# Splitting FFN weights with fewer, wider VectorE instructions, and a third seven-product pair in the long down products

## Chip, cores and metric

The kernel runs on one core of one Trainium2 chip, as one launch. The metric is the device time of that launch in microseconds (us). A run executes the program and reports its time; one more execution is recorded by the hardware profiler, and every profile row below is from such an execution.

## What is computed

A two-layer decoder trunk on 256 tokens of width 2048, in float32: a dilated-window attention layer and a latent-attention layer, each followed by a SwiGLU feed-forward block (FFN), all with RMSNorm and residuals. The change concerns the FFN, which runs once per layer:

```python
D_MODEL = 2048; SEQ = 256; FFN_HIDDEN = 5632
def swiglu(xn, w_gu, w_down):                 # xn (256, 2048), w_gu (2048, 11264), w_down (5632, 2048)
    g, u = jnp.split(xn @ w_gu, 2, axis=-1)
    return (jax.nn.silu(g) * u) @ w_down
# each layer:  h = h + attention(rms_norm(h));  h = h + swiglu(rms_norm(h, ffn_norm_g), w_gu, w_down)
```

## The kernel before

**Products in two parts.** TensorE (PE) multiplies in `float32r`, which keeps fewer bits than float32. Every weight tile `raw` is therefore split: ScalarE (ACT) rounds it to `hi` (`nc.scalar.copy` with a cast), VectorE (DVE) forms the residue `lo = raw - hi`. The activations are stored in the same way, transposed, as `xT` and `hT`. A product of a 128x128 block of x with a 128x512 block of w is three matmuls: x_hi w_hi, x_hi w_lo, x_lo w_hi (`mul` in `mixed`, lines 689 to 691). A line of the profile that names `halve` (L167 and L168) is this split in the FFN; L157 and L158 are the same split in the attention layers.

**Units and the stream.** `WeightStream` holds a list of units. In the FFN, a unit is a `raw` tile of [128, 2048]: two k blocks (rows of the weight) times two column blocks of 512, in the order b12, b11, b22, b21. Two transfers of 512 KB on the SP queue fill it. `ws.next()` hands out a unit and, before that, emits the split of the unit two places ahead (`ahead=2`) and the loads after it. There are three buffers each of `raw`, `hi` and `lo`. A `hi` buffer comes free when PE has done its last matmul with it, a `raw` buffer when DVE has read it last.

**Eight or seven products.** One unit meets a 2x2 block of x (two k blocks, two token halves), so it is a 2x2 by 2x2 block product. An "eight" unit takes eight `mul`, 24 matmuls. A "seven" unit uses a Winograd form with seven `mul`, 21 matmuls: three take the unit's own `hi` and `lo`, four take `th` and `tl`, the split of four combinations of its blocks, which DVE makes in place in `raw` (lines 185 to 188). `th` and `tl` have one buffer each. On the x side, `sums` makes the matching combinations, once for each k pair (`forms` for the gate/up products, `forms_h` for the down products). Four PSUM banks `pb` collect the shared products; after the last seven unit, line 721 combines them into the tiles `left` and `right`.

**Stages.** An FFN is worked in three parts of its hidden width, with 16, 16 and 12 blocks of 128 (`FFN_PARTS`). In a part, for each four blocks (`j`), `mixed` computes the gate and up products over eight k pairs `kp` = 0 to 7; all but the first of a layer have seven units at kp 2, 4 and 6 (`SEVEN`), and there are 20 such products in the program. Then line 739 adds the accumulators `la` (gate) and `ra` (up) to `left` and `right` ("gate add", "up add"), line 745 is the silu on ACT, line 747 multiplies on DVE, and `turned`, one unit later, transposes the result on PE into `hT` (line 405) and calls `sums` on the pairs that need it. `la` and `ra` have two buffers in PSUM together, so the next product's first matmul waits for the gate add. After the gate/up products of the two long parts come two long down products each (`mixed` again, eight k pairs, eight in the program), with seven units at kp 2 and 5; the short part's down product has none and uses other code.

**Order.** The code is written in program order and a scheduler of the language sets the order on each engine; each engine then works its own list strictly in that order and waits on semaphores of the others. An instruction that waits holds up all that stand behind it on its engine.

In what follows S2, S4 and S6 are the seven units of a gate/up product by their kp, E3, E5 and E7 the eight units between them, E0' and E1' the first two of the next product and S2' its first seven unit.

Of the kernel before, what the change touches and what calls it, by code (L numbers as in the profile page):

```python
# [48 lines left out]
SEVEN_DOWN = {16: (2, 5), 12: ()}  # L49
# [38 lines left out]
class WeightStream:  # L88
# [81 lines left out]
    def split_blocks(self, raw, form):  # L170
# [14 lines left out]
        tt(out=b22, in0=b22, in1=b12, op=ALU.subtract)  # L185
        tt(out=b12, in0=b12, in1=b11, op=ALU.subtract)
        tt(out=b11, in0=b11, in1=b22, op=ALU.add)  # L187
        tt(out=b21, in0=b21, in1=b11, op=ALU.subtract)
        for i in (slice(0, 1024), slice(1024, 2048)):
            self.halve(th[:, i], tl[:, i], raw[:, i])  # L190
# [32 lines left out]
def kernel(ctx, tc, consts, x, attn_norm_g, ffn_norm_g, a_w_qkv, a_w_o, kv_norm_g,  # L223
# [206 lines left out]
    def across(r, name):  # L430

        dg = tmp.tile([P, S], F32, tag="diag", name="diag", bufs=1)
        for t in range(NT):
            nc.vector.tensor_scalar(out=dg[:, t * P:(t + 1) * P], in0=ident, scalar1=r[:, t:t + 1],
                                    scalar2=None, op0=ALU.mult)
# [205 lines left out]
    def ffn(xT, rstd, finish):  # L641

        with tc.tile_pool(name="ffn", bufs=1) as fp:
# [11 lines left out]
            forms_h = fp.tile([P, 2, 2, 3, P], F32R, name="forms_h")  # L655

            def sums(x, kp, d):
# [7 lines left out]
                for i, x_, y_, op in ((0, a21, a22, ALU.add), (1, g[:, 0], a11, ALU.subtract),  # L665
                                      (2, a11, a21, ALU.subtract), (3, a12, g[:, 1], ALU.subtract)):
# [12 lines left out]
            def mixed(X, pairs, seven, sums_of, left, right):  # L679
# [5 lines left out]
                pb = None  # L685
# [289 lines left out]
```

## Time and profile before

| | |
|---|---|
| median of 3 runs (lowest, highest) | 2673.95 us (2673.07, 2676.16) |
| span of the profiled execution, first to last instruction | 2672.9 us |
| mean granted TensorE clock | 0.998 |
| PE busy | 2655.3 us, 99% of the span |
| DVE busy | 2020.8 us, 76% |
| ACT busy | 1295.8 us, 48% |

The profiler gives the profiled execution as its span; its time with what lies around the span is not listed apart, and the median of the runs is 1.05 us above the span. PE's busy share says little about stalls, since matmuls are pipelined: a 128x512 matmul is listed with 390 ns while the next one starts 227 ns after it. So PE is read here by starts, not by busy time. The same holds in a small way for DVE and ACT: an instruction's listed time overlaps the next one's start when the next does not need its result. The FFNs lie at about 950 to 1670 us and 1920 to 2672 us of the span.

### The profile page before, as it was taken

To read this page: it belongs to the slowest core of one execution; us is meant where nothing else is said; L and a number is where in the kernel's file an instruction comes from. 1 tells how busy PE (TensorE), PEld (TensorE's weight loads), DVE (VectorE), ACT (ScalarE), POOL (GpSimd) and SP (SyncE) were. 2 spreads that over 40 slices of the span, in tenths; PEclk is the share of its full clock that TensorE was granted. 3 is DMA by queue.
4 is the path that set the end of the run, shared out by engine and by line. 5 is a ranking of instruction groups with operands and counts; after the bars stand their busy time and mean duration, and the time that the engine had idled before them with its cause. 6 is when DMAs were issued, how large, how long until landed. Compare 5 with 4: busy or idle time off the path is not lost.

```text
span 2672.9 us, 32983 instructions
## 1 busy us (share of the span) xinstructions
PE 2655.3 (99%) x12938; PEld 2228.0 (83%) x12938; DVE 2020.8 (76%) x2758; ACT 1295.8 (48%) x1649; POOL 24.9 (1%) x28
## 2 busy tenths in 40 slices
PE   9999999999999999999999999999999999999998
PEld 7888888888888888888888888888888888888887
DVE  5676577477477668988998896588579978997985
ACT  5444444434444445544554454565445544554553
POOL 0000000000000000000000000000000000000000
PEclk9999999999999999999999999999999999999999
DMA  7545545554555555566566756444555576657663
GB/s 271 190 158 171 192 159 173 189 174 164 174 183 165 198 188 190 184 210 221 185 211 211 227 175 203 157 143 140 177 180 189 189 230 199 217 188 222 204 215 133
DMA packets 308091, 504.20 MB, mean 189 GB/s; under 512 B 13960, under 2 KB 117088, under 8 KB 307552
## 3 DMA queue, kind: packets, MB, share of 16 engines
q1 hardware_dynamic: 302960, 492.64, 55.2%
q0 software_dynamic: 4352, 8.39, 1.7%
q8 instruction: 101, 1.65, 0.3%
q10 hardware_dynamic: 624, 1.07, 0.1%
q14 instruction: 54, 0.44, 0.0%
HBM read 491.57 MB, written 2.10 MB: 185 GB/s over the span
## 4 chain that ended last, share of the span: by engine, by line
PE 87%; DVE 6%; DMA 3%; issue 2%; ACT 2%; SPq 0%; POOL 0%; ACTq 0%; DVEq 0%; POOLq 0%
PE acc L451 14%; PE acc L689 10%; PE acc L690 10%; PE acc L691 10%; PE acc L471 8%; PE acc L470 8%; PE acc L472 8%; PE acc L454 7%; DVE lo L168 2%; PE bank L689 2%; PE bank L691 2%; PE bank L690 2%; DMA raw<-in_ffn_w_gu_dram 1%; DMA raw<-in_ffn_w_down_dram 1%; PE bank L566 1%
## 5 line engine op out<-in xcount | busy, mean ns | idle before, releaser
L158 DVE TENSOR_TENSOR lo<-raw,hi 128x1024 fp32r<-128x1024 f32 (+2 forms) x450 | 515.7, 1166 | 347.3 <-ACT hi L157 331.3
L157 ACT CAST hi<-raw 128x1024 fp32r<-128x1024 f32 (+2 forms) x450 | 432.6, 1006 | 550.0 <-PE acc L451 297.4
L167 ACT CAST hi<-raw 128x1024 fp32r<-128x1024 f32 (+1 forms) x404 | 443.8, 1130 | 384.3 <-PE acc L691 146.4
L168 DVE TENSOR_TENSOR lo<-raw,hi 128x1024 fp32r<-128x1024 f32 (+1 forms) x404 | 526.2, 1321 | 110.0 <-ACT hi L167 108.8
L689 PE MATMUL acc<-hi,xT_f 128*128 128x512 f32 x988 | 387.2, 392 | 0.4 <-DVE gate L739 0.4
L691 PE MATMUL acc<-hi,xT_f 128*128 128x512 f32 x988 | 385.4, 390 | 0.0
L690 PE MATMUL acc<-lo,xT_f 128*128 128x512 f32 x988 | 385.0, 390 | 0.0
L451 PE MATMUL acc<-xT_a,hi 128*128 128x512 f32 x1536 | 379.4, 395 | 0.0
L451 PEld LDWEIGHTS acc<-xT_a,hi 128*128 128x128 f32 x1536 | 281.6, 188 | 53.8
L689 PEld LDWEIGHTS acc<-hi,xT_f 128*128 128x128 f32 x988 | 185.5, 188 | 41.8 <-issue 2.5
L167 ACT CAST th<-raw 128x1024 fp32r<-128x1024 f32 x152 | 154.0, 1049 | 133.4 <-DVE raw L187 122.3
L691 PEld LDWEIGHTS acc<-hi,xT_f 128*128 128x128 f32 x988 | 185.5, 188 | 39.1
L690 PEld LDWEIGHTS acc<-lo,xT_f 128*128 128x128 f32 x988 | 185.6, 188 | 38.2
L454 PEld LDWEIGHTS acc<-xT_a,lo 128*128 128x128 f32 x1536 | 196.9, 191 | 7.6
L454 PE MATMUL acc<-xT_a,lo 128*128 128x256 f32 x1536 | 199.2, 283 | 0.0
L168 DVE TENSOR_TENSOR tl<-raw,th 128x1024 fp32r<-128x1024 f32 x152 | 180.5, 1221 | 12.6 <-ACT th L167 12.4
L689 PE MATMUL acc<-hi,hT 128*128 128x512 f32 x400 | 156.4, 391 | 1.5 <-DVE gate L739 1.0
L691 PE MATMUL acc<-hi,hT 128*128 128x512 f32 x400 | 155.9, 390 | 0.0
L690 PE MATMUL acc<-lo,hT 128*128 128x512 f32 x400 | 155.8, 390 | 0.0
L471 PE MATMUL acc<-lo,xT_a 128*128 128x512 f32 x384 | 150.6, 392 | 0.8 <-DVE lo L158 0.8
L472 PE MATMUL acc<-hi,xT_a 128*128 128x512 f32 x384 | 150.9, 393 | 0.0
L470 PE MATMUL acc<-hi,xT_a 128*128 128x512 f32 x384 | 150.8, 393 | 0.0
(274 smaller groups left out, 3942.6 us busy)
## 6 DMA issues: line engine op xcount, KB each, us to landing
raw<-in_ffn_w_gu_dram SPq DMA_DIRECT2D x352, 512.0 KB, 4.5
raw<-in_a_w_qkv_dram SPq DMA_DIRECT2D x143, 1024.0 KB, 4.9
raw<-in_ffn_w_down_dram SPq DMA_DIRECT2D x128, 512.0 KB, 5.0
raw<-in_ffn_w_down_dram SPq DMA_DIRECT2D x24, 1024.0 KB, 5.1
raw<-in_a_w_o_dram SPq DMA_DIRECT2D x16, 1024.0 KB, 5.0
raw<-in_b_w_o_dram SPq DMA_DIRECT2D x16, 1024.0 KB, 5.1
raw<-in_b_w_kv_b_dram SPq DMA_DIRECT2D x8, 1024.0 KB, 5.3
raw<-in_b_w_q_b_dram SPq DMA_DIRECT2D x8, 768.0 KB, 4.5
```

The lines of the kernel that those rows point to most:

```text
L157: nc.scalar.copy(out=h, in_=src)
L158: nc.vector.tensor_tensor(out=l, in0=src, in1=h.bitcast(F32), op=ALU.subtract)
L167: self.nc.scalar.copy(out=hi, in_=src)
L168: self.nc.vector.tensor_tensor(out=lo, in0=src, in1=hi.bitcast(F32), op=ALU.subtract)
L451: mm(out=acc[:, i, :], lhsT=sl(hi, kk), rhs=xT[:, k0 + kk, :], start=first and kk == 0, stop=False)
L454: mm(out=acc[:, i, 0:S], lhsT=sl(lo, kk), rhs=xT[:, k0 + kk, 0:S], start=False, stop=last and kk == nk - 1)
L470: mm(out=acc[:, t, :ncol], lhsT=xh, rhs=rhs(hi, kk), start=st, stop=False)
L471: mm(out=acc[:, t, :ncol], lhsT=xh, rhs=rhs(lo, kk), start=False, stop=False)
L472: mm(out=acc[:, t, :ncol], lhsT=xl, rhs=rhs(hi, kk), start=False, stop=sp)
L689: mm(out=out, lhsT=xh, rhs=wh, start=st, stop=False)
L690: mm(out=out, lhsT=xh, rhs=wl, start=False, stop=False)
L691: mm(out=out, lhsT=xl, rhs=wh, start=False, stop=sp)
```

## The change

It has five edits.

1. `split_blocks`: an eight unit is split in one piece of 2048 columns instead of two of 1024. In a seven unit DVE first adds b11 to b12 in place (line 177), then all 2048 columns are split (before, the 1536 of b11, b22 and b21). One subtraction of 512 (line 182) and one of 1024 columns with a broadcast operand (line 183) make the three combinations, which are split in one piece of 1536 into `th` and `tl` (before, four combinations in two pieces of 1024).
2. `mixed`: of the seven `mul`, four now use the unit's own `hi` and `lo` and come first, and three use `th` and `tl`.
3. The combination after the last seven unit takes three instructions instead of four (two of 512 columns, one of 1024); `gate` has three slots of 512 in place of `gate` with two and `u2`.
4. `SEVEN_DOWN` for the long down products is (2, 4, 6) instead of (2, 5). `sums` is called for one more pair in each long part; one of its subtractions has its operands exchanged.
5. `across` builds its diagonal in `R` instead of a tile of its own.

On DVE, at the third seven unit of a gate/up product (the fourth product of a layer's first part; raw_8680 before and raw_8611 after are that S6, raw_8721 and raw_8649 the E7 behind it; line 168 is `halve` in both kernels), before:

```order
L168 TENSOR_TENSOR lo_8783<-raw_8680,hi_8782 128x1536
L185 TENSOR_TENSOR raw_8680<-raw_8680 128x512
L186 TENSOR_TENSOR raw_8680<-raw_8680 128x512
L168 TENSOR_TENSOR lo_8821<-raw_8721,hi_8820 128x1024
L187 TENSOR_TENSOR raw_8680<-raw_8680 128x512
L168 TENSOR_TENSOR lo_8821<-raw_8721,hi_8820 128x1024
L188 TENSOR_TENSOR raw_8680<-raw_8680 128x512
L168 TENSOR_TENSOR tl_8787<-raw_8680,th_8786 128x1024 x2
```

Here the pieces of E7's residue stand between the four combinations, and the first piece of `th` can be made after line 187. At the same place after:

```order
L168 TENSOR_TENSOR tl_8644<-raw_8507,th_8643 128x1536
L177 TENSOR_TENSOR raw_8611<-raw_8611 128x512
L168 TENSOR_TENSOR lo_8709<-raw_8611,hi_8708 128x2048
L182 TENSOR_TENSOR raw_8611<-raw_8611 128x512
L168 TENSOR_TENSOR lo_8744<-raw_8649,hi_8743 128x2048
L183 TENSOR_TENSOR raw_8611<-raw_8611 128x2x512
L168 TENSOR_TENSOR tl_8714<-raw_8611,th_8713 128x1536
L168 TENSOR_TENSOR lo_8775<-raw_8681,hi_8774 128x2048
```

Line 177 stands directly ahead of the residue that needs ACT's `hi` of the same tile, and line 183 directly ahead of `tl`, which needs ACT's `th`.

On ACT, where that product begins (gate_8280 before and gate_8237 after are the gate of the product that ends there; hi_8608 and hi_8544 belong to the new product's S2; lines 718 and 716 are the copy of `pb[0]`), before:

```order
L718 COPY gate_8280<-bank_8400 128x512
L167 CAST hi_8565<-raw_8472 128x1024 x2
L745 ACTIVATE gate_8280<-gate_8280,rem_7623 128x512 x2
L167 CAST hi_8608<-raw_8502 128x1536
L167 CAST hi_8674<-raw_8535 128x1024
```

and after:

```order
L716 COPY gate_8237<-bank_8349 128x512
L167 CAST hi_8503<-raw_8416 128x2048
L167 CAST hi_8544<-raw_8444 128x2048
L745 ACTIVATE gate_8237<-gate_8237,rem_7618 128x512 x2
L167 CAST hi_8607<-raw_8475 128x2048
```

S2's `hi` has moved ahead of the silu, and it is 2048 columns wide. The DMA issues on SP and POOL are the same in number and size.

```diff
-SEVEN_DOWN = {16: (2, 5), 12: ()}
+SEVEN_DOWN = {16: (2, 4, 6), 12: ()}
...
-        blk = lambda t, i: t[:, i * 512:(i + 1) * 512]
+        v = raw.rearrange("p (i c) -> p i c", c=512)
+        if form == "seven":
+            self.nc.vector.tensor_tensor(out=v[:, 0], in0=v[:, 0], in1=v[:, 1], op=ALU.add)
+        self.halve(hi, lo, raw)
         if form == "eight":
-            for i in (slice(0, 1024), slice(1024, 2048)):
-                self.halve(hi[:, i], lo[:, i], raw[:, i])
             return hi, lo
-        i = slice(512, 2048)
-        self.halve(hi[:, i], lo[:, i], raw[:, i])
-        th, tl = [self.sum_pool.tile([P, 2048], F32R, tag=n, name=n, bufs=1) for n in ("th", "tl")]
-        b12, b11, b22, b21 = [blk(raw, j) for j in range(4)]
-        tt = self.nc.vector.tensor_tensor
-        tt(out=b22, in0=b22, in1=b12, op=ALU.subtract)
-        tt(out=b12, in0=b12, in1=b11, op=ALU.subtract)
-        tt(out=b11, in0=b11, in1=b22, op=ALU.add)
-        tt(out=b21, in0=b21, in1=b11, op=ALU.subtract)
-        for i in (slice(0, 1024), slice(1024, 2048)):
-            self.halve(th[:, i], tl[:, i], raw[:, i])
+        th, tl = [self.sum_pool.tile([P, 1536], F32R, tag=n, name=n, bufs=1) for n in ("th", "tl")]
+        self.nc.vector.tensor_tensor(out=v[:, 2], in0=v[:, 0], in1=v[:, 2], op=ALU.subtract)
+        self.nc.vector.tensor_tensor(out=v[:, 1::2], in0=v[:, 1::2],
+                                     in1=v[:, 2].unsqueeze(1).broadcast_to([P, 2, 512]), op=ALU.subtract)
+        self.halve(th, tl, raw[:, 512:])
         return hi, lo, th, tl
...
-        dg = tmp.tile([P, S], F32, tag="diag", name="diag", bufs=1)
+        R = small.tile([P, S], F32, name=name, tag=name, bufs=1)
...
-        mm(out=ps[:, :S], lhsT=ones, rhs=dg, start=True, stop=True)
-        R = small.tile([P, S], F32, name=name, tag=name, bufs=1)
+        mm(out=ps[:, :S], lhsT=ones, rhs=R, start=True, stop=True)
...
-                        mul(la[:, 0], x(0, 1), w[:2], 3, False, False)
-                        mul(ra[:, 0], y(3), w[:2], 2, False, False)
-                        mul(la[:, 1], x(1, 1), w[2:], 3, False, False)
-                        mul(pb[1], y(0), w[2:], 0, st, sp)
+                        mul(la[:, 0], x(0, 1), w[:2], 3, first("la0"), False)
+                        mul(pb[1], y(0), w[:2], 0, st, sp)
+                        mul(ra[:, 0], y(3), w[:2], 2, first("ra0"), False)
+                        mul(pb[3], y(2), w[2:], 0, st, sp)
                         mul(pb[2], y(1), w[2:], 1, st, sp)
-                        mul(pb[3], y(2), w[2:], 2, st, sp)
+                        mul(la[:, 1], x(1, 1), w[2:], 2, first("la1"), False)
...
-                        for o, x_, y_ in ((u2, pb[2], left[:, 0]), (left[:, 1], pb[3], u2),
-                                          (right[:, 0], pb[1], u2), (right[:, 1], pb[1], left[:, 1])):
-                            nc.vector.tensor_tensor(out=o, in0=x_, in1=y_, op=ALU.add)
+                        nc.vector.tensor_tensor(out=left[:, 1], in0=pb[2], in1=left[:, 0], op=ALU.add)
+                        nc.vector.tensor_tensor(out=left[:, 2], in0=pb[3], in1=left[:, 1], op=ALU.add)
+                        nc.vector.tensor_tensor(out=right, in0=pb[1].unsqueeze(1).broadcast_to([P, NT, 512]),
+                                                in1=left[:, 1:3], op=ALU.subtract)
```

More of the change, by code (lines that the diff above doesn't have):

```diff
@@ L430, in across @@
     def across(r, name):
-        dg = tmp.tile([P, S], F32, tag="diag", name="diag", bufs=1)
+        R = small.tile([P, S], F32, name=name, tag=name, bufs=1)
         for t in range(NT):
-            nc.vector.tensor_scalar(out=dg[:, t * P:(t + 1) * P], in0=ident, scalar1=r[:, t:t + 1],
+            nc.vector.tensor_scalar(out=R[:, t * P:(t + 1) * P], in0=ident, scalar1=r[:, t:t + 1],
                                     scalar2=None, op0=ALU.mult)
         ps = bank()
-        mm(out=ps[:, :S], lhsT=ones, rhs=dg, start=True, stop=True)
-        R = small.tile([P, S], F32, name=name, tag=name, bufs=1)
+        mm(out=ps[:, :S], lhsT=ones, rhs=R, start=True, stop=True)
         nc.vector.tensor_copy(out=R, in_=ps[:, :S])
@@ L653, in ffn @@
             forms = fp.tile([P, len(SEVEN), 2, 3, P], F32R, name="forms")
-            forms_h = fp.tile([P, 2, 2, 3, P], F32R, name="forms_h")
+            forms_h = fp.tile([P, 3, 2, 3, P], F32R, name="forms_h")
             def sums(x, kp, d):
@@ L665, in sums @@
                 for i, x_, y_, op in ((0, a21, a22, ALU.add), (1, g[:, 0], a11, ALU.subtract),
-                                      (2, a11, a21, ALU.subtract), (3, a12, g[:, 1], ALU.subtract)):
+                                      (2, a21, a11, ALU.subtract), (3, a12, g[:, 1], ALU.subtract)):
                     nc.vector.tensor_tensor(out=g[:, i], in0=x_, in1=y_, op=op)
@@ L684, in mixed, with first @@
                 la, ra = acc_tile(), acc_tile()
-                pb = None
+                pb, begun = None, set()
+                def first(m):
+                    new = m not in begun
+                    begun.add(m)
+                    return new
                 def mul(out, x, w, i, st, sp):
@@ L702, in mixed @@
                         mul(pb[0], x(0, 0), w[:2], 1, st, sp)
-                        mul(la[:, 0], x(0, 1), w[:2], 3, False, False)
-                        mul(ra[:, 0], y(3), w[:2], 2, False, False)
-                        mul(la[:, 1], x(1, 1), w[2:], 3, False, False)
-                        mul(pb[1], y(0), w[2:], 0, st, sp)
+                        mul(la[:, 0], x(0, 1), w[:2], 3, first("la0"), False)
+                        mul(pb[1], y(0), w[:2], 0, st, sp)
+                        mul(ra[:, 0], y(3), w[:2], 2, first("ra0"), False)
+                        mul(pb[3], y(2), w[2:], 0, st, sp)
                         mul(pb[2], y(1), w[2:], 1, st, sp)
-                        mul(pb[3], y(2), w[2:], 2, st, sp)
+                        mul(la[:, 1], x(1, 1), w[2:], 2, first("la1"), False)
                     else:
-                        st, sp = kp == 0, kp == pairs - 1
-                        for acc, n in ((la, 1), (ra, 0)):
+                        sp = kp == pairs - 1
+                        for acc, m, n in ((la, "la", 1), (ra, "ra", 0)):
                             for t in range(NT):
-                                mul(acc[:, t], x(t, 0), w, n, st, False)
+                                mul(acc[:, t], x(t, 0), w, n, first(f"{m}{t}"), False)
                                 mul(acc[:, t], x(t, 1), w, n + 2, False, sp)
@@ L716, in mixed @@
                     if seven and kp == seven[-1]:
-                        u2 = fp.tile([P, 512], F32, tag="u2", name="u2")
                         nc.scalar.copy(out=left[:, 0], in_=pb[0])
-                        for o, x_, y_ in ((u2, pb[2], left[:, 0]), (left[:, 1], pb[3], u2),
-                                          (right[:, 0], pb[1], u2), (right[:, 1], pb[1], left[:, 1])):
-                            nc.vector.tensor_tensor(out=o, in0=x_, in1=y_, op=ALU.add)
+                        nc.vector.tensor_tensor(out=left[:, 1], in0=pb[2], in1=left[:, 0], op=ALU.add)
+                        nc.vector.tensor_tensor(out=left[:, 2], in0=pb[3], in1=left[:, 1], op=ALU.add)
+                        nc.vector.tensor_tensor(out=right, in0=pb[1].unsqueeze(1).broadcast_to([P, NT, 512]),
+                                                in1=left[:, 1:3], op=ALU.subtract)
                 return la, ra
             def pair_tiles():
-                return [fp.tile([P, NT, 512], F32, tag=m, name=m) for m in ("gate", "up")]
+                return [fp.tile([P, n, 512], F32, tag=m, name=m) for m, n in (("gate", NT + 1), ("up", NT))]
             for part, (k0, n) in enumerate(FFN_PARTS):
@@ L736, in ffn @@
                     g, u = mixed(xT, KD // 2, () if first else SEVEN, forms, gate, up)
+                    gate = gate[:, 0:3:2]
                     if not first:
@@ L764, in ffn @@
                                                     op=ALU.add)
-                    for i, part_sum in enumerate((left, right)):
+                    for i, part_sum in enumerate((left[:, 0:3:2], right)):
                         nc.gpsimd.dma_start(out=h[:, :, (c + i) * 512:(c + i + 1) * 512], in_=part_sum,
```

## Prediction

> **What bounds the kernel now.** I read the page first, then the busy time of one FFN product, then the three engines in order of time in that product, and last the waits.
>
> ```profile
> PE 2655.3 (99%) x12938; PEld 2228.0 (83%) x12938; DVE 2020.8 (76%) x2758; ACT 1295.8 (48%) x1649; POOL 24.9 (1%) x28
> ```
>
> By the page PE bounds everything. The window of one gate/up product (the fourth of the first part, 1107.96 to 1151.08 us) and that of two down products with the gate/up product behind them say more:
>
> ```profile
> 1107.96:1151.08 43.12, 42.80 (x193) 34.96 (x191) 41.22 (x49) 23.45 (x27) 0.00 (x0) 1.00 0.57 193
> 1151.00:1278.00 127.00, 126.92 (x561) 104.70 (x562) 104.42 (x109) 61.33 (x62) 4.96 (x4) 1.00 0.68 216
> ```
>
> The columns are the length, then busy us of PE, PEld, DVE, ACT and POOL. In the gate/up product DVE is busy 41.22 of 43.12 us (96%), in the down stretch 104.42 of 127 (82%). So in gate/up products DVE is a second bound that nearly touches PE. PE's starts in the same product:
>
> ```profile
> 1107.96 0.39 PE L689 MATMUL acc<-hi,xT_f 128*128 128x512 f32 x1
> ...
> 1113.17 0.39 PE L691 MATMUL acc<-hi,xT_f 128*128 128x512 f32 x1
> 1113.40 1.03 PE L405 MATMUL bank<-ident,up 128*128 128x128 f32 x8
> ...
> 1119.74 0.39 PE L689 MATMUL bank<-hi,xT_f 128*128 128x512 f32 x1
> ...
> 1124.58 0.39 PE L689 MATMUL acc<-hi,xT_f 128*128 128x512 f32 x1
> ...
> 1150.37 0.39 PE L691 MATMUL acc<-hi,xT_f 128*128 128x512 f32 x1
> 1151.08 0.47 PE L689 MATMUL acc<-hi,hT 128*128 128x512 f32 x1 [0.32 <-DVE gate L739]
> ```
>
> An eight unit takes 1113.40 - 1107.96 = 5.44 us (24 starts of 0.227), a seven unit 1124.58 - 1119.74 = 4.84. The transposes of line 405 stand right behind the first unit. The last gap, 0.71 us instead of 0.227, is a stall of 0.48: PE waits for the gate add. Without it the product takes 42.64 us; that is PE's own bound. Over the program such stalls are few so far:
>
> ```profile
> PE acc L689 <- DVE gate L739: 1.4, 5, 0.4
> PE acc L690 <- DVE tl L168: 0.6, 2, 0.5
> ```
>
> They name the two places at which DVE can hold PE: `tl` of a seven unit, and the gate add.
>
> **What the change removes on DVE and ACT.** Durations by form:
>
> ```profile
> L168 DVE TENSOR_TENSOR lo<-raw,hi 128x1024 fp32r<-128x1024 f32 x328 | 393.0, 1220 | 68.6 <-ACT hi L167 67.6
> L168 DVE TENSOR_TENSOR lo<-raw,hi 128x1536 fp32r<-128x1536 f32 x76 | 133.5, 1756 | 41.4 <-ACT hi L167 41.2
> L662 DVE TENSOR_TENSOR f<-hT 128x512 f32<-128x512 f32 x8 | 5.5, 682 | 0.0
> L667 DVE TENSOR_TENSOR g<-f 128x128 f32<-128x128 f32 x28 | 6.8, 285 | 0.2
> L381 DVE TENSOR_TENSOR forms_h<-g,forms_h 128x384 fp32r<-128x384 f32 x8 | 4.4, 551 | 0.0
> ...
> L167 ACT CAST hi<-raw 128x1024 fp32r<-128x1024 f32 x328 | 331.4, 1050 | 284.4 <-PE acc L691 112.0 <-DMA raw<-in_ffn_w_gu_dram 76.0 <-issue 65.3
> L167 ACT CAST hi<-raw 128x1536 fp32r<-128x1536 f32 x76 | 112.4, 1479 | 99.9 <-issue 35.3 <-PE acc L691 34.4 <-DMA raw<-in_ffn_w_down_dram 20.8
> ```
>
> From 1024 to 1536 columns DVE takes 0.536 us more and ACT 0.429. So 2048 columns, which no row shows, take 2.29 us on DVE and 1.91 on ACT; the steps of the two measured sizes bound this to some hundredths. What an instruction costs in a full queue is the time to the next start:
>
> ```profile
> 1108.16 1.22 DVE L739 TENSOR_TENSOR up<-acc,up 128x1024 f32<-128x1024 f32 x1 [0.73 <-PE acc L691]
> 1109.48 1.42 DVE L747 SCALAR_TENSOR_TENSOR up<-up,rem,gate 128x512 f32<-128x512 f32 x2
> 1110.82 1.75 DVE L168 TENSOR_TENSOR lo<-raw,hi 128x1536 fp32r<-128x1536 f32 x1
> 1112.60 0.69 DVE L185 TENSOR_TENSOR raw<-raw 128x512 f32<-128x512 f32 x1
> 1113.33 0.69 DVE L186 TENSOR_TENSOR raw<-raw 128x512 f32<-128x512 f32 x1
> ...
> 1121.73 1.75 DVE L168 TENSOR_TENSOR lo<-raw,hi 128x1536 fp32r<-128x1536 f32 x1
> 1123.40 0.48 DVE L667 TENSOR_TENSOR g<-f 128x128 f32<-128x128 f32 x2
> ...
> 1137.32 1.22 DVE L168 TENSOR_TENSOR lo<-raw,hi 128x1024 fp32r<-128x1024 f32 x1
> 1138.46 0.69 DVE L188 TENSOR_TENSOR raw<-raw 128x512 f32<-128x512 f32 x1
> 1139.06 2.43 DVE L168 TENSOR_TENSOR tl<-raw,th 128x1024 fp32r<-128x1024 f32 x2
> ...
> 1149.71 1.23 DVE L739 TENSOR_TENSOR gate<-acc,gate 128x1024 f32<-128x1024 f32 x1
> ```
>
> That is 0.60 us for 512 columns (1138.46 to 1139.06), 0.73 where the next needs the result (1112.60 to 1113.33), 1.14 for 1024, 1.67 for 1536, hence 2.20 for 2048. A seven unit costs DVE before: 1.67, four combinations at about 0.65, two pieces of `tl` at 1.15: 6.57. After: 0.60 + 2.20 + 0.60 + 1.14 + 1.67 = 6.21, less by 0.36. An eight unit goes from 2.28 to 2.20, the combination after the last seven unit loses 0.15. A gate/up product saves 3 x 0.36 + 5 x 0.08 + 0.15, about 1.6 us, and DVE's busy time falls from 41.22 to 39.6. The Trainium skill, Perfetto Trace Analysis, section Optimizing Scalar/DVE Operations, gives about 60 ns of access overhead for a VectorE instruction on SBUF; by that alone twelve instructions less would save an estimated 0.7 us.
>
> **What it adds: waits of DVE for ACT.** ACT's rows of the same product:
>
> ```profile
> 1107.52 1.34 ACT L745 ACTIVATE gate<-gate,rem 128x512 f32<-128x512 f32 x2 [5.27 <-DVE gate L739]
> 1108.77 1.47 ACT L167 CAST hi<-raw 128x1536 fp32r<-128x1536 f32 x1
> 1113.60 1.05 ACT L167 CAST hi<-raw 128x1024 fp32r<-128x1024 f32 x1 [3.37 <-PE acc L691]
> ...
> 1137.52 1.05 ACT L167 CAST th<-raw 128x1024 fp32r<-128x1024 f32 x1 [1.02 <-DVE raw L187]
> 1139.18 1.05 ACT L167 CAST th<-raw 128x1024 fp32r<-128x1024 f32 x1 [0.61 <-DVE raw L188]
> ```
>
> Before, DVE hardly waits here: at 1137.52 `th`'s first piece is made behind line 187 while DVE does E7's residue, so `tl` starts at 1139.06 without a pause. After, by the order shown above, three waits are forced, and nothing in DVE's list stands between:
> - S6's residue. Line 177 ends (0.69), ACT makes `hi` of 2048 columns (1.91), then DVE goes on: 0.69 + 0.1 + 1.91 + 0.05 less the 0.60 that line 177 costs is 2.1 us idle.
> - S6's `tl`. Line 183 ends (1.22 after its start), ACT makes `th` of 1536 columns (1.48): 0.1 + 0.1 + 1.48 is 1.65 us idle.
> - S2's residue. Its `hi` needs the buffer that PE frees with the product's last matmul (like the row at 1113.60, which starts 0.4 us after the last matmul's start at 1113.17), so it runs from 0.2 to 2.1 us after the new product's start. The up add ends at 1.4 (1109.38 - 1107.96), so DVE idles 0.7 us. The silu stands behind that `hi` and ends at 3.4; the residue occupies DVE until 4.35, line 747 until 5.7. Before, line 747 was done at 2.9. PE's transposes are due at 5.44: 0.3 us of stall.
>
> Together 39.6 + 2.1 + 1.65 + 0.7 and 0.3 for the up add's own start and dependent steps gives 44.35 us against PE's 42.64. From the other side: laid out in that order, `tl` of S6 ends 35.7 us after the product's start (before: 1141.5, which is 33.5), where PE wants it at 35.5; then two residues of 2.20, the three combinations (0.6, 0.6, 1.15), one line 177 and the gate add (1.25) end at 44.4. PE can't start the next product earlier. A product with `sums` in it takes 44.4 instead of 43.1: +1.3. The waits alone can't take less than the instruction that is waited for, 1.91 + 1.48 less what DVE could be late anyway; the ends are 0 (DVE has slack everywhere) and +3 (the waits come on top of all the idle time that there is, 43.12 - 41.22 = 1.9).
>
> Products without `sums` (0.68 + 4 x 0.285 + 0.28 + 0.55, less overlaps, about 2.5 us of DVE) are not 2.5 better: S4's `hi` can't start before PE has finished the second unit at about 12.0, and `th` of S4 holds `tl` by another 1.0. The same layout gives 43.5, where such a product takes about 42.9: +0.6. The row `f<-hT` x8 says that 8 of the 20 products have `sums`; so 8 x 1.3 + 12 x 0.6 = +17.6 us. In the four gate/up products that follow down products no transposes are due and the product starts with DVE less late; I take 0.3 off each: +16.4.
>
> **The down products.** Eight units become seven units: 8 x (5.44 - 4.84) = -4.8 us of PE. DVE does a seven unit more in each (6.21 - 2.20 = 4.0) and four `sums` more, all in the first down product of a part; that one has 42.0 us of PE work and lands, laid out in the same way, 0.8 us late: 4 x 0.8 = +3.2. In the second, without `sums`, the residues lead by some 2 us: nothing. Net -1.6. If DVE's slack (127 - 104.42 = 22.6 us over three products) covers everything, -4.8; if nothing, +3.
>
> **Edits at nothing.** ACT's busy time falls (23.45 of 43.12), hidden anyway. Exchanged operands cost what they did. `across` in one tile: its four calls lie ahead of the products that use them; uncovered, a few tenths. Loads on SP and the accumulating DMA on POOL keep number and size; SP's load of a unit waits for DVE's last read of the buffer:
>
> ```profile
> raw<-in_ffn_w_gu_dram SPq DMA_DIRECT2D x352, 512.0 KB, 4.5
> ```
>
> and the longest wait for a load on the chain that ended last:
>
> ```profile
> 1434.57 7.40 DMA raw<-in_ffn_w_down_dram
> ```
>
> E7's load follows E5's residue (at 21.7 in the layout), lands 4.5 to 5 later and has its `hi` by 28.6; DVE wants it at 28.95. It just fits; with the 7.4 us of the longest row it does not.
>
> The sum against the profiled execution: 2672.9 + 16.4 - 1.6 = 2687.7 of span, and 1.05 more for the median: about 2688 us.
>
> **Rivals.** *Faster: DVE is relieved.* An engine at 96% gets twelve instructions less per product; if the waits fall into the 1.9 us in which it idles now, PE stalls less. The sum is then -4.8 and the stalls of today: 43.12 - 42.64 = 0.5 in products with `sums`, some 0.25 in others, 8 x 0.5 + 12 x 0.25 = 7. That gives 2662, or 2669 with the PE part alone. It decides if the three waits are under 42.64 - 39.6 = 3.0 us; I count 4.45. The Trainium skill, Perfetto Trace Analysis, section Optimizing Scalar/DVE Operations, takes this side: grouping into larger operations can improve throughput if the engine is saturated; the same section says that where an engine is not saturated but causes bubbles on others, breaking instructions up may let work end sooner, which is my forecast. The window's 96% speaks for the first, the ACT row at 1137.52 for the second.
>
> *A wash.* The waits come out at 3.3 us: 0.25 x 20 = +5 cancels -4.8, 2674. For it speaks that each of my layouts could be half a microsecond too long.
>
> *Much slower: loads join.* S6's tile is held longer, E7's and the next first units' `raw` land late as in the 7.40 row, 1 us more in each of 20 products: about 2708. Against it: the median landing.
>
> **How the numbers follow.** Forecast (slower by some 5 to 25 us) 0.52, much slower 0.08, wash 0.16, faster 0.24. A measurement of this kernel tells a change from none at about 0.2%, 5.3 us. The layout's error of 0.7 us a product makes 14 us either way around 2688; the faster case lies at 2662 to 2668. The range 2664 to 2704 leaves out the best tenth and the worst tenth; the likeliest case alone is 2679 to 2700.
>
> **What would show it.** Right: idle time of DVE before `lo` and `tl` of line 168 put down to ACT grows by tens of microseconds (3.5 us times 20 products), and PE's waits for the gate add or `tl` grow; DVE's busy time in a product falls to about 39.6; gate adds follow each other at 43.5 to 44.5 us; a stretch of two down products and a gate/up product is shorter than 127 by about 1. Wrong: gate adds at 42.6 or less. Most likely to break the forecast is the slack: if DVE runs ahead of PE, forced waits cost nothing.

## The result, and the profile after

The changed kernel takes 2701.89 us (median of 4 runs, 2699.3 to 2704.41), the kernel before 2673.61 us (4 runs, 2673.07 to 2676.16). The ratio is 1.0107, 95% interval 1.0093 to 1.0121: slower by 28.3 us, where 14 were forecast. In what follows "with sums" and "without" mean gate/up products with and without `sums` in them, and a *down stretch* is the time from the last gate add of a long part to the next gate add: two down products and one gate/up product. There are four.

First the page of the kernel after: its engines, then the chain of work that ended last, by engine and by line.

```profile
PE 2658.6 (98%) x12914; PEld 2222.5 (82%) x12914; DVE 2021.7 (75%) x2474; ACT 1287.4 (48%) x1425; POOL 25.0 (1%) x28
...
PE 72%; DVE 14%; DMA 6%; ACT 5%; issue 3%; SPq 0%; ACTq 0%; DVEq 0%; POOL 0%; POOLq 0%
PE acc L445 14%; DVE lo L168 8%; PE acc L465 8%; PE acc L464 8%; PE acc L466 8%; PE acc L448 7%; PE acc L688 7%; PE acc L690 6%; PE acc L689 6%; ACT hi L167 4%; DMA raw<-in_ffn_w_down_dram 4%; DMA raw<-in_ffn_w_gu_dram 1%; PE bank L560 1%; PE bank L400 1%; PE bank L690 1%
```

The same chain of the kernel before:

```profile
PE 87%; DVE 6%; DMA 3%; issue 2%; ACT 2%; SPq 0%; POOL 0%; ACTq 0%; DVEq 0%; POOLq 0%
PE acc L451 14%; PE acc L689 10%; PE acc L690 10%; PE acc L691 10%; PE acc L471 8%; PE acc L470 8%; PE acc L472 8%; PE acc L454 7%; DVE lo L168 2%; PE bank L689 2%; PE bank L691 2%; PE bank L690 2%; DMA raw<-in_ffn_w_gu_dram 1%; DMA raw<-in_ffn_w_down_dram 1%; PE bank L566 1%
```

The busy shares hardly differ, and DVE works through 284 instructions less. The chain shows the change: PE's share falls from 87% to 72%, and `lo` of line 168, `hi` of line 167 and the loads of the down weights take its place. A glance at the busy line alone would have called the two kernels equal.

The waits of the kernel after (total us, times, longest):

```profile
DVE lo L168 <- ACT hi L167: 114.9, 105, 3.3
DVE tl L168 <- ACT th L167: 51.5, 34, 1.6
PE acc L688 <- DVE gate L739: 19.1, 18, 1.8
PE bank L689 <- DVE tl L168: 6.1, 8, 1.3
PE acc L688 <- DVE h L763: 5.0, 8, 0.9
```

PE waits for DVE in three places, 19.1 + 6.1 + 5.0 = 30.2 us; before, the gate add, `tl` and the `h` add cost it 1.4 + 0.6 + 0.4 = 2.4. The difference is 28 us. PE also has 24 matmuls less to do, which the prediction puts at 4.8 us, so it must have lost some 34 us more than before in all: these three places are most of it. Eight of the waits for `tl` and eight of those for the `h` add (line 763, the end of a down product) fit the eight long down products.

Gate adds mark the program well (DVE's rows `gate<-acc,gate`). From one to the next, mean us of one trace each:

| | before | after | difference, times its number |
|---|---|---|---|
| product with sums (8) | 43.19 | 44.36 | +1.17 x 8 = +9.4 |
| product without, between two gate adds (6) | 42.96 | 43.33 | +0.37 x 6 = +2.2 |
| down stretch (4) | 127.30 | 131.56 | +4.27 x 4 = +17.1 |
| ahead of the first gate add, and between the layers | | | +1.0 |

That adds up to the 29.7 us by which the spans differ (2702.6 and 2672.9). The windows of one product with sums (gate add to gate add) and of the down stretch behind it, kernel after, with the columns of the prediction's windows:

```profile
1109.09:1153.30 44.21, 42.91 (x192) 35.08 (x191) 39.49 (x36) 22.81 (x18) 0.00 (x0) 1.00 0.56 187
1153.30:1285.08 131.78, 126.91 (x556) 103.12 (x556) 110.34 (x90) 62.83 (x42) 5.00 (x4) 1.00 0.66 209
```

In the product DVE is busy 39.49 us (41.22 before) and the product is longer. In the down stretch DVE has 21.4 us left over, and the stretch is 4.3 us longer although PE has six matmuls less to do in its two down products (24 over the program, by the page's counts).

DVE's rows of the kernel after, first in the product, then in the second down product behind it; the bracket is the idle time ahead of a row and what ended it:

```profile
1133.28 0.68 DVE L177 TENSOR_TENSOR raw<-raw 128x512 f32<-128x512 f32 x1
1135.98 2.29 DVE L168 TENSOR_TENSOR lo<-raw,hi 128x2048 fp32r<-128x2048 f32 x1 [2.02 <-ACT hi L167]
...
1141.12 1.22 DVE L183 TENSOR_TENSOR raw<-raw 128x1024 f32<-128x1024 f32 x1
1143.96 1.76 DVE L168 TENSOR_TENSOR tl<-raw,th 128x1536 fp32r<-128x1536 f32 x1 [1.62 <-ACT th L167]
...
1150.78 0.68 DVE L718 TENSOR_TENSOR gate<-bank,gate 128x512 f32<-128x512 f32 x1
1151.38 0.68 DVE L177 TENSOR_TENSOR raw<-raw 128x512 f32<-128x512 f32 x1
1151.98 1.22 DVE L719 TENSOR_TENSOR up<-bank,gate 128x1024 f32<-128x1024 f32 x1
1153.30 1.23 DVE L739 TENSOR_TENSOR gate<-acc,gate 128x1024 f32<-128x1024 f32 x1
...
1203.63 0.69 DVE L177 TENSOR_TENSOR raw<-raw 128x512 f32<-128x512 f32 x1 [2.30 <-DMA raw<-in_ffn_w_down_dram]
...
1225.21 2.29 DVE L168 TENSOR_TENSOR lo<-raw,hi 128x2048 fp32r<-128x2048 f32 x1 [2.02 <-ACT hi L167]
...
1233.93 1.76 DVE L168 TENSOR_TENSOR tl<-raw,th 128x1536 fp32r<-128x1536 f32 x1 [1.62 <-ACT th L167]
```

The two waits of S6 stand there with 2.02 and 1.62 us (forecast 2.1 and 1.65). The third forced wait, 0.7 us at S2's residue with 0.3 at the transposes, did not come: ACT starts that `hi` at 1109.24, before the product's first matmul at 1110.46, because PE itself is held there. E3's residue waits 0.85 us instead (1118.17). Two things were not priced by themselves in the forecast. Line 177 of the *next* product's S2 stands ahead of line 719 and the gate add (1151.38): 0.6 us of DVE's time at the place that PE waits for. And at 1203.63 line 177 waits 2.30 us for a load, with all that is queued behind it. PE's rows at which DVE held it up, at the start of that product, at its end, and in the down products:

```profile
1110.46 0.47 PE L688 MATMUL acc<-hi,xT_f 128*128 128x512 f32 x1 [1.30 <-DVE gate L739]
...
1154.67 0.47 PE L688 MATMUL acc<-hi,hT 128*128 128x512 f32 x1 [1.25 <-DVE gate L739]
...
1191.53 0.50 PE L689 MATMUL bank<-tl,forms_h 128*128 128x512 f32 x1 [1.23 <-DVE tl L168]
...
1199.69 0.47 PE L688 MATMUL acc<-hi,hT 128*128 128x512 f32 x1 [0.57 <-DVE h L763]
...
1235.75 0.50 PE L689 MATMUL bank<-tl,forms_h 128*128 128x512 f32 x1 [1.30 <-DVE tl L168]
...
1243.90 0.47 PE L688 MATMUL acc<-hi,xT_f 128*128 128x512 f32 x1 [0.53 <-DVE h L763]
```

Each of the two down products stalls PE at a `tl` and at its end, 3.6 us in all. What DVE is late for shows in the chain of 1150 to 1290 us: first its shares by line, then rows of it (start, us, what):

```profile
by line: DVE lo L168 27.4%; DMA raw<-in_ffn_w_down_dram 19.9%; ACT hi L167 13.7%; issue 10.5%; PE acc L688 4.7%; PE acc L690 4.2%; PE acc L689 4.2%; DVE raw L183 3.4%; DVE up L719 2.5%; DVE raw L177 1.9%; DVE gate L739 1.8%; SPq L106 1.3%; 
...
1160.43 1.92 ACT hi L167
1162.38 2.30 DVE lo L168
1164.69 0.37 SPq L106
...
1165.11 5.18 DMA raw<-in_ffn_w_down_dram
...
1170.38 1.92 ACT hi L167
...
1174.43 2.21 DVE lo L168
...
1177.11 5.51 DMA raw<-in_ffn_w_down_dram
...
1182.73 1.92 ACT hi L167
1184.67 2.29 DVE lo L168
```

It is a ring: a load is issued when a residue `lo` has ended, lands 5.2 to 5.5 us later, ACT rounds the whole tile in 1.92, DVE takes the residue in 2.2 to 2.3, and the next load goes out. The ring turns in some 12 us (1164.69 to the end of `lo` at 1176.64), and there `lo`, the loads and `hi` have 61% of the chain, PE some 13%. One turn brings two units, since only every second `lo` stands on it (between those of 1162.38 and 1174.35 lies one at 1168.78). For a seven and an eight unit PE needs 4.84 + 5.44 = 10.3 us; from the end of one such `lo` to the end of the next the chain takes 12.0 (1164.68 to 1176.64), 10.3 (to 1186.96) and, in the second down product, 10.2 and 10.3. So by these rows the ring is as long as PE's own work or longer, and what lengthens it delays PE. DVE's 21 us of idle time are the pauses in that ring, and so cover little.

### The profile page after: what moved, and what is told of

Same layout as the page of the kernel before. It is cut to its first block, busy times and chain, and to the rows that moved or that the text cites. A ratio compares the mean times of both kernels' runs of the same rounds, so it can differ in the third digit from the quotient of the medians.

```text
span 2702.6 us, 32462 instructions
## 1 busy us (share of the span) xinstructions
PE 2658.6 (98%) x12914; PEld 2222.5 (82%) x12914; DVE 2021.7 (75%) x2474; ACT 1287.4 (48%) x1425; POOL 25.0 (1%) x28
## 3 DMA queue, kind: packets, MB, share of 16 engines
q8 instruction: 101, 1.65, 0.2%
## 4 chain that ended last, share of the span: by engine, by line
PE 72%; DVE 14%; DMA 6%; ACT 5%; issue 3%; SPq 0%; ACTq 0%; DVEq 0%; POOL 0%; POOLq 0%
PE acc L445 14%; DVE lo L168 8%; PE acc L465 8%; PE acc L464 8%; PE acc L466 8%; PE acc L448 7%; PE acc L688 7%; PE acc L690 6%; PE acc L689 6%; ACT hi L167 4%; DMA raw<-in_ffn_w_down_dram 4%; DMA raw<-in_ffn_w_gu_dram 1%; PE bank L560 1%; PE bank L400 1%; PE bank L690 1%
## 5 line engine op out<-in xcount | busy, mean ns | idle before, releaser
L167 ACT CAST hi<-raw 128x2048 fp32r<-128x2048 f32 x240 | 458.9, 1912 | 499.9 <-PE acc L690 216.2
L168 DVE TENSOR_TENSOR lo<-raw,hi 128x2048 fp32r<-128x2048 f32 x240 | 549.4, 2289 | 116.9 <-ACT hi L167 114.9
L167 ACT CAST th<-raw 128x1536 fp32r<-128x1536 f32 x84 | 124.0, 1476 | 154.3 <-DVE raw L183 154.3
L168 DVE TENSOR_TENSOR tl<-raw,th 128x1536 fp32r<-128x1536 f32 x84 | 147.4, 1754 | 51.5 <-ACT th L167 51.5
L688 PE MATMUL acc<-hi,hT 128*128 128x512 f32 x344 | 135.2, 393 | 8.0 <-DVE gate L739 5.2
L689 PE MATMUL acc<-lo,hT 128*128 128x512 f32 x344 | 134.3, 390 | 0.0
L690 PE MATMUL acc<-hi,hT 128*128 128x512 f32 x344 | 134.0, 390 | 0.0
```

Of the source, the lines that this page charges most:

```text
L167: self.nc.scalar.copy(out=hi, in_=src)
L168: self.nc.vector.tensor_tensor(out=lo, in0=src, in1=hi.bitcast(F32), op=ALU.subtract)
L688: mm(out=out, lhsT=xh, rhs=wh, start=st, stop=False)
L689: mm(out=out, lhsT=xh, rhs=wl, start=False, stop=False)
L690: mm(out=out, lhsT=xl, rhs=wh, start=False, stop=sp)
```

## The experiments

Medians in us, ratios against the kernel before on the same chip with 95% intervals, and the same three periods. "e10 again" is the same kernel in another session; the periods come from one trace each, and those of the two e10 differ by up to 0.3 us.

| kernel | median | ratio | with sums | without | down stretch |
|---|---|---|---|---|---|
| before | 2673.6 | 1 | 43.19 | 42.96 | 127.30 |
| after | 2701.9 | 1.0107 (1.0093 to 1.0121) | 44.36 | 43.34 | 131.56 |
| e1, after with two pairs | 2696.2 | 1.0088 (1.0071 to 1.0105) | 44.50 | 43.33 | 129.39 |
| e2, before with the third pair | 2669.8 | 0.9987 (0.9977 to 0.9996) | 42.99 | 42.90 | 126.76 |
| e3, after with narrow pieces | 2690.7 | 1.0066 (1.0051 to 1.0081) | 43.51 | 43.48 | 129.91 |
| e5, after with a late sum | 2701.5 | 1.0108 (1.0093 to 1.0123) | 43.91 | 43.72 | 131.28 |
| e6, after without the accumulating DMA | 2701.7 | one run | 44.30 | 43.33 | 131.24 |
| e7, e2 with wide eights | 2676.8 | 1.0020 (1.0011 to 1.0030) | 43.24 | 42.82 | 127.77 |
| e8, e3 with a late sum | 2694.4 | 1.0085 (1.0067 to 1.0102) | 43.72 | 43.46 | 129.96 |
| e10, e2 with the wide combination | 2666.8 | 0.9981 (0.9971 to 0.9991) | 42.89 | 42.79 | 126.32 |
| e10 again | 2669.9 | 0.9987 (0.9978 to 0.9996) | 43.20 | 42.82 | 126.50 |
| e11, e10 and 0.6 us ahead of the gate add | 2681.0 | 1.0028 (1.0016 to 1.0039) | 43.32 | 43.14 | 127.93 |
| e12, e8 with three products on `hi` | 2693.4 | 1.0074 (1.0061 to 1.0088) | 43.73 | 43.30 | 130.34 |
| e13, e12 without line 177 | 2676.7 | 1.0015 (1.0006 to 1.0024) | 43.22 | 42.96 | 127.94 |

**The third pair, taken back and done alone.** e1 is the kernel after with the pairs of before:

```diff
-SEVEN_DOWN = {16: (2, 4, 6), 12: ()}
+SEVEN_DOWN = {16: (2, 5), 12: ()}
```

> The changed kernel with seven units at kp 2 and 5 of the long down products again, as before the change; the wide splits stay. Theory A (in the down products the third seven unit overloads the chain of waits and loads): the stretch from the last gate add of a long part to the next one falls from about 131.6 us to about 128, four times, and the time from 2702 to about 2687. Rival B (the wide splits alone slow the down products): the stretch stays at 130 or more, and since PE has 1.2 us more to do in it, the time stays at 2699 to 2706.

e2 is the kernel before with only this line (and edit 5, which makes room) the other way round.

> The kernel before with seven units at kp 2, 4 and 6 of the long down products, split in the old narrow pieces (and the diagonal built in R, for room). Theory A (the third seven unit overloads the chain whatever the splits): the down stretch grows from 127.3 us to 129 or more, the time to 2680 or more. Rival B (the old splits have slack there: DVE idles 22 us in 127): the stretch falls by 1.2 us, PE's saving, and the time to about 2669.

On the old splits the third pair gains: 2669.8, about 3 of the 4.8 us that PE's matmuls alone would give. On the new ones it costs: the kernel after is 5 to 6 us slower than e1. The two intervals overlap a little, but the down stretches, the only place that the edit touches, differ by 2.2 us each the wrong way. Same edit, other sign. The chain of e1 says what it meets there:

```profile
PE 78%; DVE 12%; ACT 4%; issue 3%; DMA 2%; SPq 0%; POOL 0%; DVEq 0%; ACTq 0%; POOLq 0%
```

With two pairs PE has 78% of the chain and DMA 2%, where after had 72% and 6%: that fits a ring which the third pair tightens, but no run shows the ring apart from the pair. But even with two pairs a down stretch takes 129.4, 2.1 us more than before, so the third pair is only part of the loss.

**Narrow pieces.** e3 keeps the new form and cuts its instructions as before cut them:

```diff
-        self.halve(hi, lo, raw)
+        for i in (slice(0, 1024), slice(1024, 2048)):
+            self.halve(hi[:, i], lo[:, i], raw[:, i])
...
-        self.halve(th, tl, raw[:, 512:])
+        for i in (slice(0, 1024), slice(1024, 1536)):
+            self.halve(th[:, i], tl[:, i], raw[:, 512:][:, i])
```

> The changed kernel with each split in two pieces again (hi and lo 1024 + 1024, th and tl 1024 + 512); the fewer combinations, the new order of products and the three pairs stay. Theory A (the waits of DVE for whole pieces of ACT cost the time): gate adds follow each other at 42.9 to 43.4 instead of 43.6 to 44.5, the time falls by 10 to 20 us to 2682 to 2692. Rival B (the wait comes from line 177, which stands ahead of hi, not from the width): the periods stay at 43.5 or more, the time above 2695.

2690.7, 11.2 us less than after, with 324 DVE instructions more. Products with sums lose 0.85 us, down stretches 1.65. So the width of the pieces costs 11 us, and the rest stays: e3 is 20.9 us slower than e2, which ran beside it and differs from it in the new form of the seven units, with its order of products, and the three-instruction combination.

e7 asks for the width alone, on the old form:

```diff
         if form == "eight":
-            for i in (slice(0, 1024), slice(1024, 2048)):
-                self.halve(hi[:, i], lo[:, i], raw[:, i])
+            self.halve(hi, lo, raw)
             return hi, lo
```

> The kernel before with three pairs in the long down products (the run at 2669.8) and only the eight units split in one piece of 2048; the seven units keep their old form. If wide eight units are harmless or good (DVE saves 5 x 0.08 us a product): 2665 to 2670. If the residue that waits for a whole hi, and the raw buffer that comes free later, cost time, as the chain of the changed kernel says: gate adds 0.2 to 0.6 us further apart, down stretch 127.5 to 129, time 2675 to 2690.

2676.8: 7 us more than e2, from which it differs in the wide eight units alone (the intervals do not meet), and 10 more than e10, which ran beside it. DVE's busy time fell by 4 to 5 us with it. The Trainium skill, Perfetto Trace Analysis, section Optimizing Scalar/DVE Operations, says that grouping can help an engine that is saturated, and that breaking instructions up can help where it is not and makes others wait. The runs side with the second: with 41.22 of 43.12 us busy in a product before, DVE looked saturated, and yet its waits for `hi` rose from 68.8 us in e2 to 89.6 in e7. By the first rule the kernel would have become faster.

**The wait behind line 177.** My theory then was that ACT loses its lead because `hi` can't start before line 177. e5 makes `hi` and `lo` of the 1536 untouched columns first, and sums afterwards:

```diff
-        if form == "seven":
-            self.nc.vector.tensor_tensor(out=v[:, 0], in0=v[:, 0], in1=v[:, 1], op=ALU.add)
-        self.halve(hi, lo, raw)
         if form == "eight":
+            self.halve(hi, lo, raw)
             return hi, lo
+        self.halve(hi[:, 512:], lo[:, 512:], raw[:, 512:])
+        self.nc.vector.tensor_tensor(out=v[:, 0], in0=v[:, 0], in1=v[:, 1], op=ALU.add)
+        self.halve(hi[:, :512], lo[:, :512], raw[:, :512])
```

> The changed kernel with line 177 moved: in a seven unit hi and lo of b11, b22 and b21 (1536 columns) are made first, as before the change, then b11 is added to b12 and the sum is split as a piece of 512. All pieces stay wide otherwise. Theory A (ACT must wait for DVE to reach line 177, so its hi loses its lead): DVE's wait of 2.1 us at S6 shrinks to under 1, gate adds come 0.5 to 1 us closer (43.5 instead of 44.4 with sums), the down stretch falls from 131.6 to about 129.5, the time to 2680 to 2690. Rival B (the width of the pieces and the late th do it, not line 177): the periods move by under 0.3 us and the time by under 6, since DVE and ACT have one piece more each.

e8 does the same with narrow pieces, on e3.

> Line 177 late as in e5 and eight units and th in two pieces as in e3. If line 177 and the widths together are the whole loss, the periods are those of the run with the third pair alone (42.95 and 126.8) and the time is 2668 to 2674, the order of the seven products and the two wide combinations being harmless. If either of these costs too (th needs line 183 whole before it starts, where the old form could start after two of four combinations), the time stays above 2677.

Neither gains: 2701.5 against 2701.9, and 2694.4 against 2690.7. The theory fell. Rows of e5, first one of ACT and then DVE's, show where the wait went:

```profile
1142.68 1.91 ACT L167 CAST hi<-raw 128x2048 fp32r<-128x2048 f32 x1 [2.96 <-PE acc L691]
...
1144.62 2.29 DVE L168 TENSOR_TENSOR lo<-raw,hi 128x2048 fp32r<-128x2048 f32 x1 [2.61 <-ACT hi L167]
...
1150.62 0.68 DVE L180 TENSOR_TENSOR raw<-raw 128x512 f32<-128x512 f32 x1
1151.21 1.22 DVE L720 TENSOR_TENSOR up<-bank,gate 128x1024 f32<-128x1024 f32 x1
1152.54 1.23 DVE L740 TENSOR_TENSOR gate<-acc,gate 128x1024 f32<-128x1024 f32 x1
```

The sum (line 180 here) has left S6's residue, which waits 0.36 us in this product, and `tl` waits for nothing. But DVE then waits 2.61 us for the `hi` of the unit behind, which ACT, idle for 2.96 us, starts only when PE is done with a matmul, and the next product's sum still stands ahead of the gate add. So the wait moved; these runs do not give its price.

**The accumulating DMA.** The down stretches contain the DMA that adds `left` and `right` to `h` on POOL's queue. e6 leaves it out.

```diff
-                    for i, part_sum in enumerate((left[:, 0:3:2], right)):
-                        nc.gpsimd.dma_start(out=h[:, :, (c + i) * 512:(c + i + 1) * 512], in_=part_sum,
-                                            accum_op=ALU.add)
```

> The changed kernel without the accumulating DMA of the down products (the parts in left and right are not added to h, so that part of the sum is left out). If that transfer makes the loads of the down weights land late (5.2 to 6.5 us instead of 4.5), the down stretch falls from 131.6 to about 129.5, the time by 5 to 10 us. If the loads are late because their buffers come free late, the stretch stays within 0.5 us and the time within 3.

2701.7 in its one run, with a stretch of 131.24: no part of the loss is seen to come from it.

**The wide combination.** e10 is e2 with the change's three-instruction combination.

```diff
-                        u2 = fp.tile([P, 512], F32, tag="u2", name="u2")
                         nc.scalar.copy(out=left[:, 0], in_=pb[0])
-                        for o, x_, y_ in ((u2, pb[2], left[:, 0]), (left[:, 1], pb[3], u2),
-                                          (right[:, 0], pb[1], u2), (right[:, 1], pb[1], left[:, 1])):
-                            nc.vector.tensor_tensor(out=o, in0=x_, in1=y_, op=ALU.add)
+                        nc.vector.tensor_tensor(out=left[:, 1], in0=pb[2], in1=left[:, 0], op=ALU.add)
+                        nc.vector.tensor_tensor(out=left[:, 2], in0=pb[3], in1=left[:, 1], op=ALU.add)
+                        nc.vector.tensor_tensor(out=right, in0=pb[1].unsqueeze(1).broadcast_to([P, NT, 512]),
+                                                in1=left[:, 1:3], op=ALU.add)
```

> The kernel before with three pairs and, of the wide edits, only the combination behind the last seven unit in three instructions. DVE saves 0.15 us a product, just ahead of the gate add for which PE waits: the time is 2666 to 2670, not more than 1 us from the run with the third pair alone (2669.8) by the rival that PE is no longer held there.

> The run at 2666.8 (old splits, three pairs, three-instruction combination) once more, in five rounds, for its interval: ratio to the kernel before 0.996 to 0.999, 2664 to 2670.

0.9981 and 0.9987, e2 0.9987: the combination does no harm, and no gain of it over e2 is shown. e10 is faster than both kernels of this case, by 3 to 5 us against before. Its page:

```profile
PE 2648.7 (99%) x12914; PEld 2222.7 (83%) x12914; DVE 2061.4 (77%) x2798; ACT 1311.8 (49%) x1665; POOL 24.9 (1%) x28
...
PE 94%; DVE 2%; DMA 1%; ACT 1%; issue 1%; SPq 0%; POOL 0%; POOLq 0%; ACTq 0%; DVEq 0%
```

Its DVE is busy 40 us *longer* than that of the kernel after, and the kernel is 32 to 35 us faster.

**What 0.6 us ahead of the gate add costs.** e11 repeats one 512-column instruction of that combination:

```diff
-                        nc.vector.tensor_tensor(out=left[:, 2], in0=pb[3], in1=left[:, 1], op=ALU.add)
+                        for _ in range(2):
+                            nc.vector.tensor_tensor(out=left[:, 2], in0=pb[3], in1=left[:, 1], op=ALU.add)
```

> The run at 2666.8 with one of its combinations of 512 columns done twice: 0.6 to 0.73 us more of DVE directly ahead of the gate add, where line 177 of the next product's first seven unit stands in the changed kernel. Theory C (whatever DVE does between E1's residue and the gate add delays PE one for one): gate adds 0.3 to 0.6 us further apart (42.84 to 43.2 to 43.4), down stretch up by 1 to 1.5, time 2677 to 2686. Rival D (DVE has slack there; the up add waited 0.2 us for PE): under 0.2 us a product, time 2667 to 2671.

2681.0 against 2669.9 for e10 beside it: +11.1 us for 28 instructions of 0.6 us (16.8 us of DVE's time). Twenty of them stand ahead of gate adds, eight ahead of the `h` adds that end the long down products. PE's waits for the gate add in e11, and in e10 beside it:

```profile
PE acc L688 <- DVE gate L740: 7.7, 18, 2.3
```

```profile
PE acc L688 <- DVE gate L739: 2.4, 6, 0.8
```

That is 5.3 of the 11 us. Gate adds lie 0.1 to 0.4 us further apart than in the two traces of e10, the down stretches 1.4 to 1.6; which waits make up the rest was not taken apart. Two thirds of the added time reach the clock, so at these places DVE has little slack in the old form either. So line 177, which the new form puts there, has a price without any wait for ACT.

**Four products on `hi`.** Another rival was that four `mul` instead of three hold the unit's own `hi` and `lo`. e12 gives e8 the old three:

```diff
-                        mul(pb[1], y(0), w[:2], 0, st, sp)
                         mul(ra[:, 0], y(3), w[:2], 2, first("ra0"), False)
+                        mul(pb[1], y(0), w[2:], 0, st, sp)
```

> The run e8 (2694.4) with three products of a seven unit on hi and four on th in the old order: the product that takes the sum b11 + b12 on the x side y0 uses a block of th instead, so that product is not the reference's. PE frees a seven unit's hi after 9 matmuls instead of 12, 0.68 us earlier. Theory C (hi of E1' waits for that, then its residue, then the gate add): gate adds 0.4 to 0.7 us closer (43.5 to 42.9-43.1), time 2676 to 2684. Rival D (hi comes free in time anyway): the periods stay within 0.2 us, time above 2690.

2693.4 against 2694.4: this rival fell.

**Without line 177.** e13 is e12 without the sum; all else stays.

```diff
         self.halve(hi[:, 512:], lo[:, 512:], raw[:, 512:])
-        self.nc.vector.tensor_tensor(out=v[:, 0], in0=v[:, 0], in1=v[:, 1], op=ALU.add)
         self.halve(hi[:, :512], lo[:, :512], raw[:, :512])
```

> The run e12 without line 177 (b11 is not added to b12, so the products that need the sum use b12 alone). If the early use of hi by a fourth product and line 177 ahead of the gate add are the whole loss of the new seven form, the periods are those of the run at 2666.8 (42.84 and 126.3) or less, since DVE has less to do: 2662 to 2670. If the time stays above 2675, something else of the new form costs: the wide broadcast subtraction, or th that waits for it.

2676.7: 16.7 us less than e12, for 84 instructions of 0.6 us. The end of a product in e8, and then in e13:

```profile
1148.71 0.68 DVE L721 TENSOR_TENSOR gate<-bank,gate 128x512 f32<-128x512 f32 x1
1149.31 0.68 DVE L181 TENSOR_TENSOR raw<-raw 128x512 f32<-128x512 f32 x1
1149.91 1.22 DVE L722 TENSOR_TENSOR up<-bank,gate 128x1024 f32<-128x1024 f32 x1
1151.23 1.23 DVE L742 TENSOR_TENSOR gate<-acc,gate 128x1024 f32<-128x1024 f32 x1
```

```profile
1147.46 0.68 DVE L720 TENSOR_TENSOR gate<-bank,gate 128x512 f32<-128x512 f32 x1
1148.18 1.22 DVE L721 TENSOR_TENSOR up<-bank,gate 128x1024 f32<-128x1024 f32 x1
1149.51 1.23 DVE L741 TENSOR_TENSOR gate<-acc,gate 128x1024 f32<-128x1024 f32 x1
```

PE's waits for DVE in e12, and then in e13:

```profile
PE acc L691 <- DVE gate L742: 9.4, 17, 1.1
PE acc L691 <- DVE h L766: 7.6, 8, 3.2
```

```profile
PE acc L690 <- DVE gate L741: 2.3, 6, 0.6
PE acc L690 <- DVE h L765: 1.5, 4, 0.5
```

Of the 17 us, 13.2 are PE's waits at these two places, the gate add, ahead of which line 177 of the next unit stood, and the end of a down product. The two waits for `hi` ahead of that gate add are the same in both, 1.62 and 1.13 us in e12, 1.62 and 1.15 in e13, so there it is the place of the sum and not a shorter wait that gains. Over the program DVE waits 163.6 us for `hi` in e13, as long as for `hi` and `th` together in the kernel after (166.4), and e13 is 25 us faster: the sum of DVE's waits does not give the loss. e13 takes away the sum's time, its place and ACT's wait for it together; elsewhere in the product these were not parted. e13 is still 6.8 us slower than e10 beside it. What remains of the new form there, above all one broadcast subtraction in place of two and with it a `th` that starts in one go, was not taken apart; this part stays open. Nor was it tried to keep line 177 and place it behind the gate add.

**The account.** From before to after: the third pair -3, the combination nothing measurable, the new form of the seven units in narrow pieces +21 (e3 against e2; in e8's form of the splits, which is 4 us slower than e3, line 177 is 17 of it and 7 are open), and wide pieces +11. That is +29, where 28.3 were measured; each ratio's interval is some 0.1% (3 us) either way, so the fit to 1 us is in part chance.

## Why the prediction was half right

The measured 2701.9 lies within the stated range, but 2 us from its upper end and outside the likeliest case (2679 to 2700). The range was drawn from the layout's error in gate/up products; that it also held the loss in the down products was luck.

- **Direction and mechanism of the gate/up products: right.** The layout had `tl` of S6 end 35.7 us after the product's start and the gate add at 44.4. In the trace the product's first matmul starts at 1110.46; `tl` ends at 1145.7, which is 35.3, and the gate add at 1154.5, which is 44.1; the next product starts 44.2 behind. The price of a product with sums came out at +1.17 (forecast +1.3), of one without at +0.37 (+0.6). Outside the down stretches the gate/up products cost 12.6 us; the forecast was 16.4 less 4 x 0.3 = 15.2.
- **The forced waits: right in size, too simple as a cause.** 2.1 and 1.65 became 2.02 and 1.62; the 0.7 at S2 did not come. That waits for whole pieces cost time is borne out by e3, which takes 0.85 of the 1.17 back. But e5 took both waits of S6 away in the product shown and gained nothing, since DVE then waited elsewhere. Part of the gate/up loss is the *place* of line 177 (e11, e13): the layout had it in the row of work ahead of the gate add ("one line 177"), so the 44.4 came out, but the prediction named only the waits as the cost.
- **"DVE idle before `lo` and `tl` grows by tens of microseconds": half.** Before `tl` it went from 12.4 to 51.5, before `lo` from 108.8 to 114.9 only. Waits that were there before went, new ones came.
- **DVE's merges: right, and of no use.** 2.29 and 1.91 us for 2048 columns were measured as 2289 and 1912 ns (mean of 240 each). DVE's busy time in a product fell from 41.22 to 39.49, forecast 39.6.
- **The down products: the term that failed.** "Net -1.6", with "the residues lead by some 2 us: nothing" for the second down product. With the +0.3 for the gate/up product that each stretch holds, the forecast for the four stretches is -0.4 ("shorter than 127 by about 1" does not follow from the sum either); measured was +17.1. Two terms were mis-sized. The new splits, put at next to nothing there, cost 2.1 us a stretch with two pairs already (e1). The third pair, at -1.6 in all, cost another 2.2 a stretch. On the old splits it gains: PE's -4.8 is there in part (e2, -3). The worst end of +3, "if nothing" is covered, does not follow from its own figures: eight seven units more at 4.0 and four `sums` at 2.5 are 42 us of DVE. Wrong was the step that DVE's slack of 22.6 us could only cover the rest or not: the chain shows that slack as idle time inside the ring of load, `hi` and `lo`. Narrow pieces take 1.65 us off a stretch (e3), leaving out line 177 takes off 2.4 (e13 against e12); line 177 waits for loads there (2.30 us at 1203.63). That the third seven unit lengthens the ring once more fits e1's chain and is not shown apart.
- **The rivals.** "Much slower: loads join", 0.08, named the right mechanism in the wrong place: loads joined the chain, but in the eight long down products, not in each of 20 gate/up products. Its evidence against, a median landing of 4.5 us, was that of the gate/up weights; the loads of down weights in the chain above land in 5.2 and 5.5 us, and they are issued only when a `lo` has ended. "Faster: DVE is relieved" fell with the result, and e3 and e7 say why: it is the narrow kernel that is faster.

## What to carry to other kernels

Idle time of an engine covers new work only if it is not the engine's share of a ring with others: before counting on slack, follow the chain through one stage and see whether load, first engine and second engine take turns. Wider instructions lower an engine's busy time and lengthen each hand-over, and between two engines that feed each other the hand-over is what counts (here 11 us). And look for what stands directly ahead of the instruction that frees an accumulator: there 28 instructions of 0.6 us cost 11 us on an engine that is idle almost a quarter of the span.

## What the runs showed of the hardware

Little was unexpected. Instruction times went on in a straight line to a size that no row had shown (2048 columns: 2289 ns on DVE, 1912 on ACT), so here they could be extrapolated; what could not was the sign of one and the same edit, the third pair, which gained 3 us in one kernel and cost 5 to 6 in the other.
